# The first matrix of the last feed-forward stage with tokens as standing operand, two of its eight pairs of rows as seven products, and its product turned by TensorE

## The chip, the cores and the metric

The kernel runs on one core of one Trainium2 chip. The metric is the time of one execution on the device in microseconds, the median of several runs. The engines are called PE (TensorE, matmul; PEld its loading of the standing operand), DVE (VectorE), ACT (ScalarE), POOL (GpSimd) and SP (SyncE, which issues the DMA).

## The reference, cut to what matters

Two layers, 256 tokens, width 2048: a retention mixer and a feed-forward stage, then a gated short convolution and a second feed-forward stage, which is the last stage, and a final norm.

```python
def swiglu(h, w_in, w_out):
    a, b = jnp.split(h @ w_in, 2, axis=-1)
    return (jax.nn.silu(a) * b) @ w_out
...
        h = (rms_norm(x, norm2_g[i]) * (1.0 + sc2) + sh2).astype(x.dtype)
        x = (x + g2 * swiglu(h, ffn_w_in[i], ffn_w_out[i])).astype(x.dtype)
    return rms_norm(x, final_g).astype(x.dtype)
```

`w_in` is 2048 x 11264 (5632 columns of a, 5632 of b), `w_out` 5632 x 2048; everything is float32.

## The kernel before, in words

A float32 factor is split in two float32r parts, hi (ACT copies the raw tile into it) and lo (DVE subtracts hi from the raw tile), and a product is made of three: hi x hi, hi x lo, lo x hi. Activations lie as rows of 128 features: `h[k]` has 128 partitions, its hi and lo part, and 256 tokens.

*Products by columns.* `product` (its two matmuls are L422 and L425) takes a 128x128 block of weights as standing operand and streams the 256 tokens of a row past it: one matmul of 512 columns (hi of the weight with hi and lo of the tokens) and one of 256 (lo of the weight). Sixteen rows sum up to one 128-wide column of the output, which lies with its features on partitions.

*Products by tokens.* `by_token` (`thrice`, L435 to L437) takes 128 tokens of a row as standing operand and streams 512 columns of weights past it: six matmuls of 512 columns for a 128x512 block of weights and 256 tokens. The output has tokens on partitions, four banks for two halves of the tokens and two column blocks (`ours`).

*Sevens.* A `Seven` is a pair of rows with two column blocks, seen as a 2x2 product (halves of the tokens and rows, rows and column blocks), made as 7 products in place of 8 (Strassen's form in Winograd's order): 21 matmuls of 512 columns in place of 24. It needs three differences of weights per pair (DVE, L366, L370, L372), four sums of activations per pair (`s1` to `s4`, made once), and four more banks, which `mixed_sums` folds (L1211 to L1214).

*Weights.* All weights lie in DRAM in the order of their use, in chunks of 128x2048 (1 MB). `fetch` brings one into one of three raw buffers (`raw`); `prepare` makes of it two pieces of 128x1024, or for a seven four (1024, 1024, 1024, 512), each a hi (L377, ACT) and a lo (L380, DVE) in one of four buffers. The order of PE is that of the code; on DVE and ACT a scheduler fills in the rest. `ahead_now` says how many pieces are prepared ahead of the one that PE uses: two, and three (`AHEAD + 1`) while the second matrix of the last stage runs. Every engine works its queue in order.

*The last stage.* The 5632 hidden features are 44 tiles of 128, in two parts of 22. A part first makes its 44 columns of the first matrix by columns (`swiglu_in`: a column of a, one of b, `summed` by ACT and DVE, silu, multiplication, `split` into hi and lo: `mid`). In part 0 the first six columns run inside `normed`, which makes `h` beside them, and after each of the next eight a `turn` brings a quarter of x to tokens on partitions (four transposes, L1104, a copy by ACT, L1105). Then the part's 22 rows of the second matrix run by tokens (`last_output`): two groups of 1024 columns, each 11 pairs of rows, of which pairs 1, 4 and 7 are sevens (`SEVEN`), 255 matmuls. `maker` makes the sums of activations for them. At a group's end DVE adds the banks (L1291), multiplies by the gate and adds to x (`gated`, L1171 and L1172); in part 1 ACT sums squares and DVE multiplies by the gain (L1297). In the very last group the last six rows of each column block come apart (`TAIL_ROWS`).

PSUM has eight banks; a group of the second matrix uses all of them.

Of the kernel before, what the change touches and what calls it, by code (L numbers as in the profile page):

```python
# [17 lines left out]
P = 128  # L18
# [22 lines left out]
SEVEN, BESIDE_CB = (1, 4, 7), 88  # L41
# [119 lines left out]
def last_out(ks, last):  # L161

    out = []
    for c in range(0, D, 2 * DV):
        cols, pairs = [c, c + DV], [ks[i : i + 2] for i in range(0, len(ks), 2)]
        rest = []
        if last and c + 2 * DV == D:
            n = TAIL_ROWS // 2
            rest = [Group([col], DV, ks=ks[-TAIL_ROWS:]) for col in cols]
            pairs = pairs[:-n]  # L170
        out.append([(Seven if i in SEVEN else lambda c, k: Group(c, DV, ks=k))(cols, k) for i, k in enumerate(pairs)])
        out[-1] += rest
    return out


LAST_OUT = [last_out(ks, i == 1) for i, ks in enumerate(halves(DFF))]


def in_use_order():
# [10 lines left out]
    for layer in range(DEPTH):  # L190
# [5 lines left out]
        for part in range(2):  # L196
            for g in FFN_IN[part]:
                yield "ffn_w_in", layer, g
            for g in sum(LAST_OUT[part], []) if layer == DEPTH - 1 else FFN_OUT[part]:
                yield "ffn_w_out", layer, g  # L200
# [31 lines left out]
def trunk(ctx: ExitStack, tc: tile.TileContext, x_in, c_in, pos_in, w_mod, cols_in, gain_in, tab_in, w_all, out):  # L232
# [803 lines left out]
    def swiglu_in(layer, part, acc, mid, beside=(), made=split):  # L1036

        pending, done, beside = [], 0, list(beside)
        for i, g in enumerate(FFN_IN[part]):
            pending += [sums(g)] if part or i else normed(acc, layer, 1, g)  # L1040
            while len(pending) >= 2:
                a, b = pending[:2]
                pending = pending[2:]
                s = a()
                g1 = tmp("silu", pool=mpool, bufs=2)
                nc.scalar.activation(g1, s, AF.Silu)
                s = b()
                m = tmp("m", pool=mpool, bufs=2)
                nc.vector.tensor_tensor(m, s, g1, op=ALU.mult)
                made(mid[done], m)  # L1050
                done += 1
            if beside and i:
                beside.pop(0)()
        assert not beside

    def mids():
        return [mpool.tile([P, 2, S], F32R, tag=f"mid{i}", name=name("mid")) for i in range(FT // 2)]

    for part in range(2):
        mid = mids()  # L1060
        swiglu_in(0, part, acc, mid)
# [32 lines left out]
    first_mid = mids()  # L1094
# [20 lines left out]
    def maker(mid):  # L1115
        kept, count = {}, [0]

        def made(dst, m):
            i = count[0]
            count[0] += 1  # L1120
            if i // 2 not in SEVEN:
                split(dst, m)
                return
            kept[i] = m
            if i % 2 == 0:
                split(dst[:, :, :P], m[:, :P])
                return
            split(dst, m)
            (a11, a21), (a12, a22) = [(v[:, :P], v[:, P:]) for v in (kept[i - 1], m)]
            u = tmp("u512", (P, DV), pool=mpool, bufs=3)  # L1130
            s1, s2, s4, s3 = [u[:, n * P : (n + 1) * P] for n in range(4)]
            nc.vector.tensor_tensor(s3, a11, a21, op=ALU.subtract)
            nc.vector.tensor_tensor(s1, a21, a22, op=ALU.add)
            nc.vector.tensor_tensor(s2, s1, a11, op=ALU.subtract)
            nc.vector.tensor_tensor(s4, a12, s2, op=ALU.subtract)
            split(mid[i - 1][:, :, P:], s3)
            split(tokens_sums[SEVEN.index(i // 2)], u[:, : 3 * P])
# [205 lines left out]
```

## Time and profile before

| | |
|---|---|
| median of three runs | 2611.96 us (2611.22 to 2614.11) |
| the profiled execution | 2613.33 us |
| its span, first to last instruction | 2611.6 us |
| PE, PEld, DVE, ACT, POOL busy | 2580.2, 2278.1, 2060.3, 1271.9, 131.6 us |
| HBM read | 685.08 MB, 263 GB/s over the span |
| granted clock of PE | 0.998 |

The profile is of one execution; times are in microseconds from the span's start. A group's mean is the time from start to end of one instruction; matmuls are pipelined, so the next starts before the one ahead has ended, and what a matmul costs is the distance of two starts. L numbers are lines of the kernel before; in the changed kernel the same code has higher numbers (L380 is L405 there, L422 is L447, L435 is L460, L366 is L391, L377 is L402, L487 is L512, L1211 is L1241, L1291 is L1315 in the first matrix and L1363 in the second).

### The profile page before, as it was taken

The page shows a single profiled execution, that of the slowest core. Times are in us where ns is not written, and L with a number is a line of the kernel's source. Part 1 is how long each engine was busy: PE and PEld are TensorE (multiplying, and loading weights), DVE is VectorE, ACT ScalarE, POOL GpSimd, SP SyncE. Part 2 cuts the span into 40 slices and gives each one's busy share as a digit, 9 for nine tenths or more (in the row PEclk, how much of TensorE's full clock was granted, in tenths as well). Part 3 has the DMA queues.
Part 4 walks back from the last instruction along what each step waited for, and adds up shares of the span by engine and source line. Part 5 has one row for each costly group of instructions (what it writes and reads, how often), then busy time and mean ns, then how long its engine had stood idle before and what let it go on. Part 6 is the DMA issues. An engine that isn't in the chain of part 4 may idle for free.

```text
span 2611.6 us, 37574 instructions
## 1 busy us (share of the span) xinstructions
PE 2580.2 (99%) x14831; PEld 2278.1 (87%) x14831; DVE 2060.3 (79%) x2622; ACT 1271.9 (49%) x1824; POOL 131.6 (5%) x232
## 2 busy tenths in 40 slices
PE   7999999999999999999999999999999999999998
PEld 6898889888899888888888898888998888888886
DVE  7988978887698888777778889888965568665678
ACT  5544543444456444344444454444564554445444
POOL 0000000110000001100001000000000000000001
PEclk9999999999999999999999999999999999999999
DMA  9976668867686888787788768887755555555554
GB/s 397 387 289 225 254 250 295 303 248 276 241 307 247 331 320 309 296 300 289 295 296 296 290 233 323 319 292 280 291 180 187 186 210 191 210 186 187 191 209 145
DMA packets 96692, 689.64 MB, mean 264 GB/s; under 512 B 10737, under 2 KB 12161, under 8 KB 13441
## 3 DMA queue, kind: packets, MB, share of 16 engines
q1 hardware_dynamic: 96514, 687.23, 71.4%
q8 instruction: 116, 1.90, 0.3%
q14 instruction: 62, 0.51, 0.1%
HBM read 685.08 MB, written 2.11 MB: 263 GB/s over the span
## 4 chain that ended last, share of the span: by engine, by line
PE 91%; DVE 4%; DMA 3%; issue 1%; ACT 1%; POOL 0%; ACTq 0%; POOLq 0%; DVEq 0%
PE bank L422 40%; PE bank L425 21%; PE bank L436 6%; PE bank L435 6%; PE bank L437 6%; DMA raw<-w_all 2%; PE bank L471 2%; PE bank L470 2%; PE bank L469 2%; DVE lo L380 1%; PE bank L602 1%; PE bank L604 1%; PE bank L603 1%; DMA raw<-w_mod 1%; DVE raw L730 1%
## 5 line engine op out<-in xcount | busy, mean ns | idle before, releaser
L380 DVE TENSOR_TENSOR lo<-raw,hi 128x1024 fp32r<-128x1024 f32 (+1 forms) x924 | 1117.6, 1215 | 461.7 <-ACT hi L377 458.2
L377 ACT CAST hi<-raw 128x1024 fp32r<-128x1024 f32 (+1 forms) x924 | 957.9, 1045 | 1012.8 <-PE bank L422 430.8
L422 PE MATMUL bank<-h,hi 128*128 128x512 f32 x3296 | 1143.9, 390 | 0.0
L425 PE MATMUL bank<-h,lo 128*128 128x256 f32 x3296 | 929.4, 282 | 0.0
L422 PEld LDWEIGHTS bank<-h,hi 128*128 128x128 f32 x3296 | 618.8, 188 | 129.4
L425 PEld LDWEIGHTS bank<-h,lo 128*128 128x128 f32 x3296 | 622.9, 189 | 0.0
L293 DVE SCALAR_TENSOR_TENSOR raw<-raw,cb 128x2048 f32<-128x2048 f32 x160 | 365.8, 2286 | 30.6 <-DMA raw<-w_mod 30.2
L422 PE MATMUL bank<-mid,hi 128*128 128x512 f32 x922 | 319.8, 390 | 0.0
L425 PE MATMUL bank<-mid,lo 128*128 128x256 f32 x922 | 260.1, 282 | 0.9 <-DVE lo L380 0.9
L422 PEld LDWEIGHTS bank<-mid,hi 128*128 128x128 f32 x922 | 173.1, 188 | 36.2
L435 PE MATMUL bank<-hi,h 128*128 128x512 f32 x512 | 201.7, 394 | 1.4 <-DVE rm L714 1.4
L436 PE MATMUL bank<-lo,h 128*128 128x512 f32 x512 | 200.6, 392 | 0.8 <-DVE lo L380 0.8
L437 PE MATMUL bank<-hi,h 128*128 128x512 f32 x512 | 199.7, 390 | 0.0
L425 PEld LDWEIGHTS bank<-mid,lo 128*128 128x128 f32 x922 | 174.3, 189 | 1.2 <-DVE lo L380 1.2
L422 PE MATMUL bank<-rm,hi 128*128 128x512 f32 x496 | 172.5, 390 | 0.0
L471 PE MATMUL bank<-h,lo 128*128 128x256 f32 x512 | 146.5, 286 | 4.4 <-DVE lo L380 4.4
L469 PE MATMUL bank<-h,hi 128*128 128x256 f32 x512 | 145.9, 285 | 3.3 <-ACT h L758 3.3
L470 PE MATMUL bank<-h,hi 128*128 128x256 f32 x512 | 145.9, 285 | 0.7 <-DVE h L759 0.7
L425 PE MATMUL bank<-rm,lo 128*128 128x256 f32 x496 | 139.8, 282 | 0.0
L436 PE MATMUL bank<-lo,mid 128*128 128x512 f32 x304 | 118.5, 390 | 1.3 <-DVE lo L380 1.2
L435 PE MATMUL bank<-hi,mid 128*128 128x512 f32 x304 | 118.4, 389 | 0.0
L437 PE MATMUL bank<-hi,mid 128*128 128x512 f32 x304 | 118.3, 389 | 0.0
(218 smaller groups left out, 2820.4 us busy)
## 6 DMA issues: line engine op xcount, KB each, us to landing
raw<-w_all SPq DMA_DIRECT2D x456, 1024.0 KB, 4.9
raw<-w_mod SPq DMA_DIRECT2D x192, 1024.0 KB, 5.4
x<-x_in SPq DMA_DIRECT2D x4, 512.0 KB, 5.7
out<-xt SPq DMA_DIRECT2D x4, 512.0 KB, 3.0
decay<-tab_in SPq DMA_DIRECT2D x8, 128.0 KB, 2.4
x<-gate_row SPq DMA_DIRECT2D x2, 512.0 KB, 4.6
last_gain<-gain_in SPq DMA_DIRECT2D x1, 1024.0 KB, 4.2
cols<-cols_in SPq DMA_DIRECT2D x1, 152.0 KB, 8.9
```

Source lines behind the costliest of these rows:

```text
L293: nc.vector.scalar_tensor_tensor(raw, raw, 1.0, cb, op0=ALU.mult, op1=ALU.mult, accum_out=total)
L377: nc.scalar.copy(hi, raw)
L380: nc.vector.tensor_tensor(lo, raw, hi.bitcast(F32), op=ALU.subtract)
L422: nc.tensor.matmul(pt, hi, h, start=fresh and k == g.ks[0], stop=False, skip_group_check=True)
L425: nc.tensor.matmul(pt[:, 1, :], lo, h[:, 0, :], start=False, stop=last and k == g.ks[-1], skip_group_check=True)
L435: nc.tensor.matmul(o, hi, w_hi, start=first, stop=False)
L436: nc.tensor.matmul(o, hi, w_lo, start=False, stop=False)
L437: nc.tensor.matmul(o, lo, w_hi, start=False, stop=last)
L469: nc.tensor.matmul(pt, hi, h[:, 0, :], start=first, stop=False, skip_group_check=True)
L470: nc.tensor.matmul(pt, hi, h[:, 1, :], start=False, stop=False, skip_group_check=True)
L471: nc.tensor.matmul(pt, lo, h[:, 0, :], start=False, stop=last, skip_group_check=True)
L602: nc.tensor.matmul(pt, hi, high, start=k == 0, stop=False, skip_group_check=True)
```

## The change

Of the 44 tiles 40 are now made by tokens too, in ten groups of four tiles (a column block of 512 of a, the same of b). Part 0 has 20 tiles, part 1 24 (`LAST_TILES`). Tiles 16 to 19 are still made by columns, six columns in the norm and two after it, with four turns of x after each of the two (`first_rows`). Then `made_in_sums` makes the sums over h for the sevens (pairs 3 and 5 of the eight pairs of rows, `IN_SEVEN`), and four groups follow in part 0, six in part 1. A group's end folds and adds the banks, takes the silu and multiplies, which gives four tiles with tokens on partitions. Ahead of the third pair of the next group (`TURNS_AT`, also if that is one of the second matrix) PE turns them with eight transposes (L1329), ACT and DVE split the result (L1333, L1334), and for the pairs of rows that are sevens in the second matrix `tokens_sums_of` makes the sums. The sevens of the second matrix are pairs 2, 4 and 6 of a group (`OUT_SEVEN`), in part 0 of ten pairs, in part 1 of twelve; part 0's last pairs come in the order 8, 6, 9, 5, 7. `ahead_now` is three from the first group on and is not set back. `h` of the last stage lies 120 elements higher, and small tiles that only take up space have other sizes.

```diff
-SEVEN, BESIDE_CB = (1, 4, 7), 88
+IN_SEVEN, OUT_SEVEN, TURNS_AT, BESIDE_CB, BESIDE_SUMS = (3, 5), (2, 4, 6), 2, 40, 48
+LAST_TILES = 20, 24
...
+def last_in():
+    n, rows = LAST_TILES[0], [(i, [2 * i, 2 * i + 1]) for i in range(KT // 2)]
+    cols = [part * DFF + j * P for j in range(n - 4, n) for part in range(2)]
+    firsts = [Group(cols[:LEAD])] + [Group([c]) for c in cols[LEAD:]]
+    fours = [[*range(0, n - 4, 4)], [*range(n, FT, 4)]]
+    return firsts, [[in_pairs([j * P, DFF + j * P], rows, IN_SEVEN) for j in js] for js in fours]
...
+    h = rows_at(EARLIER)
...
-        swiglu_in(1, part, acc, mid, () if part else turns, maker(mid))
...
+    def tokens_sums_of(a11, a21, a12, a22, third, others):
+        u = tmp("u512", (P, DV), pool=mpool, bufs=3)
+        s1, s2, s4, s3 = [u[:, n * P : (n + 1) * P] for n in range(4)]
+        nc.vector.tensor_tensor(s3, a11, a21, op=ALU.subtract)
+        nc.vector.tensor_tensor(s1, a21, a22, op=ALU.add)
+        nc.vector.tensor_tensor(s2, s1, a11, op=ALU.subtract)
+        nc.vector.tensor_tensor(s4, a12, s2, op=ALU.subtract)
+        split(third, s3)
+        n = 3 * P // len(others)
+        for i, dst in enumerate(others):
+            split(dst, u[:, i * n : (i + 1) * n])
...
+    def made_in_sums():
...
+        for i in IN_SEVEN:
+            both = tmp("u512", (P, 2, S), pool=mpool, bufs=3)
+            for n in range(2):
+                k = 2 * i + n
+                high, low = [h[k].bitcast(F32)[:, v, :] for v in range(2)]
+                nc.vector.tensor_tensor(both[:, n, :], high, low, op=ALU.add)
...
+            tokens_sums_of(*parts(both), h[2 * i][:, :, P:], in_sums[i])
...
-    def last_output(part, c, groups, act, base):
...
+    def gathered(groups, act, base, sums, beside=None, mixed=None):
         ours = {(t, j): flat_bank() for t in range(2) for j in range(2)}
...
+        banks, n = [], len(sums)
         for i, g in enumerate(groups):
+            if beside:
+                beside(i)
+            if i == TURNS_AT and waiting:
+                waiting.pop(0)()
             if isinstance(g, Seven):
                 n -= 1
+                banks = banks or [flat_bank() for _ in range(4)]
...
+    def last_input(groups, pairs, seven):
+        ours, extra = gathered(groups, h, 0, in_sums)
+        for (t, j), pt in ours.items():
+            nc.vector.tensor_tensor(extra[t, j], pt, extra[t, j], op=ALU.add)
+        ms = []
+        for t in range(2):
+            m = extra[t, 0]
+            nc.scalar.activation(m, m, AF.Silu)
+            nc.vector.tensor_tensor(m, m, extra[t, 1], op=ALU.mult)
+            ms.append(m)
+        def turned():
+            for n, (dst, of) in enumerate(zip(pairs, seven)):
+                pt = bank()
+                for i in range(2):
+                    for t, m in enumerate(ms):
+                        c = slice((2 * n + i) * P, (2 * n + i + 1) * P)
+                        nc.tensor.transpose(pt[:, i, t * P : (t + 1) * P], m[:, c], ident)
+                if of is not None:
+                    both = tmp("u512", (P, 2, S), pool=mpool, bufs=3)
+                    nc.scalar.copy(both, pt)
+                nc.scalar.copy(dst[:, :, 0, :], pt)
+                nc.vector.tensor_tensor(dst[:, :, 1, :], pt, dst[:, :, 0, :].bitcast(F32), op=ALU.subtract)
+                if of is not None:
+                    tokens_sums_of(*parts(both), dst[:, 0, :, P:], [of])
+        waiting.append(turned)
...
+        if not part:
+            first_rows(mid[-2:])
+            made_in_sums()
+            ahead_now[0] = AHEAD + 1
+        for i, groups in enumerate(LAST_IN[part]):
...
+            last_input(groups, mid[2 * i : 2 * i + 2], seven)
```

On PE, at the end of a column of part 0 before the change; the first operand is the row of h or the weight that stands or streams, `hi` and `lo` the pieces of weights:

```order
L422 MATMUL bank_3716_20196<-h_97,hi_3708_20162 128x512
L425 MATMUL bank_3716_20196<-h_97,lo_3709_20163 128x256
L422 MATMUL bank_3716_20196<-h_97,hi_3708_20162 128x512
L425 MATMUL bank_3716_20196<-h_97,lo_3709_20163 128x256
L422 MATMUL bank_3722_20239<-h_97,hi_3718_20199 128x512
L425 MATMUL bank_3722_20239<-h_97,lo_3719_20200 128x256
```

And after it, around the transposes of a group's product (`x12` is the tile that holds it now, `tab` the identity), ahead of the third pair of the next group:

```order
L460 MATMUL bank_3522_19114<-hi_3523_19115,h_97 128x512
L461 MATMUL bank_3522_19114<-lo_3524_19116,h_97 128x512
L462 MATMUL bank_3522_19114<-hi_3523_19115,h_97 128x512
L1329 MATMUL bank_3533_19184<-tab_78,x12_76 128x128 x4
L1329 MATMUL bank_3534_19191<-tab_78,x12_76 128x128 x4
L460 MATMUL bank_3519_19111<-hi_3526_19133,h_97 128x512
L461 MATMUL bank_3519_19111<-lo_3527_19134,h_97 128x512
L462 MATMUL bank_3519_19111<-hi_3526_19133,h_97 128x512
L460 MATMUL bank_3521_19113<-hi_3526_19133,h_97 128x512
```

One pair of matmuls for a block of weights has become three for each bank, and between two pairs of rows stand eight transposes.

On DVE, two columns of a and b before the change, from their weights' lo to their split product:

```order
L380 TENSOR_TENSOR lo_3486_18907<-raw_3484_18904,hi_3485_18906 128x1024
L380 TENSOR_TENSOR lo_3488_18927<-raw_3484_18904,hi_3487_18926 128x1024
L481 TENSOR_TENSOR sum_3490_18948<-bank_3476_18854,low_3489_18946 128x256
L380 TENSOR_TENSOR lo_3499_18970<-raw_3497_18967,hi_3498_18969 128x1024
L380 TENSOR_TENSOR lo_3501_18990<-raw_3497_18967,hi_3500_18989 128x1024
L481 TENSOR_TENSOR sum_3493_18954<-bank_3483_18903,low_3492_18952 128x256
L1049 TENSOR_TENSOR m_3494_18956<-sum_3493_18954,silu_3491_18950 128x256
L487 TENSOR_TENSOR mid_3331_18097<-m_3494_18956,mid_3331_18097 128x256
```

And after it, the end of a group of four tiles (`bank` L1315 are its four banks, L1320 the product with the silu), with the lo pieces of the next group between:

```order
L405 TENSOR_TENSOR lo_3573_19379<-raw_3571_19376,hi_3572_19378 128x1024
L405 TENSOR_TENSOR lo_3575_19395<-raw_3571_19376,hi_3574_19394 128x1024
L1315 TENSOR_TENSOR x12_76<-bank_3519_19111,x12_76 128x512
L405 TENSOR_TENSOR lo_3578_19413<-raw_3576_19410,hi_3577_19412 128x1024
L1315 TENSOR_TENSOR u512_3567_19353<-bank_3520_19112,u512_3567_19353 128x512
L1315 TENSOR_TENSOR x12_76<-bank_3521_19113,x12_76 128x512
L1315 TENSOR_TENSOR u512_3568_19354<-bank_3522_19114,u512_3568_19354 128x512
L1320 TENSOR_TENSOR x12_76<-x12_76,u512_3567_19353 128x512
L1320 TENSOR_TENSOR x12_76<-x12_76,u512_3568_19354 128x512
L405 TENSOR_TENSOR lo_3584_19441<-raw_3576_19410,hi_3583_19440 128x1024
L405 TENSOR_TENSOR lo_3587_19459<-raw_3585_19456,hi_3586_19458 128x1024
L391 TENSOR_TENSOR x8_75<-raw_3590_19490 128x1024
```

What was one sum a column with two lo pieces between is now four adds and two multiplications in a row, once for eight columns.

On DVE, where the second matrix of part 0 begins, before the change (the first seven is the second pair):

```order
L380 TENSOR_TENSOR lo_3779_20543<-raw_3777_20540,hi_3778_20542 128x1024
L487 TENSOR_TENSOR mid_3346_18112<-m_3769_20492,mid_3346_18112 128x256
L370 TENSOR_TENSOR raw_3798_20609<-raw_3798_20609,x8_75 128x512
L380 TENSOR_TENSOR lo_3781_20563<-raw_3777_20540,hi_3780_20562 128x1024
L481 TENSOR_TENSOR sum_3783_20584<-bank_3770_20496,low_3782_20582 128x256
L380 TENSOR_TENSOR lo_3800_20613<-raw_3798_20609,hi_3799_20612 128x1024
L372 TENSOR_TENSOR raw_3798_20609<-raw_3798_20609 128x512
L380 TENSOR_TENSOR lo_3802_20617<-x8_75,hi_3801_20616 128x1024
L481 TENSOR_TENSOR sum_3786_20590<-bank_3776_20539,low_3785_20588 128x256
L1049 TENSOR_TENSOR m_3787_20592<-sum_3786_20590,silu_3784_20586 128x256
L380 TENSOR_TENSOR lo_3804_20634<-raw_3798_20609,hi_3803_20633 128x1024
```

And after it, around the transposes that stand ahead of its third pair, which is the first seven; the lo pieces of the pair behind it are the last two rows:

```order
L405 TENSOR_TENSOR lo_3727_20218<-raw_3711_20133,hi_3726_20217 128x512
L1142 TENSOR_TENSOR u512_3720_20196<-u512_3719_20192 128x128
L1143 TENSOR_TENSOR u512_3720_20196<-u512_3719_20192 128x128
L1334 TENSOR_TENSOR mid_3332_18098<-bank_3718_20187,mid_3332_18098 128x2x256
L1144 TENSOR_TENSOR u512_3720_20196<-u512_3720_20196,u512_3719_20192 128x128
L1334 TENSOR_TENSOR mid_3333_18099<-bank_3721_20205,mid_3333_18099 128x2x256
L1145 TENSOR_TENSOR u512_3720_20196<-u512_3719_20192,u512_3720_20196 128x128
L391 TENSOR_TENSOR x8_75<-raw_3733_20249 128x1024
L512 TENSOR_TENSOR mid_3332_18098<-u512_3720_20196,mid_3332_18098 128x128
L512 TENSOR_TENSOR sums_of_tokens_18107<-u512_3720_20196,sums_of_tokens_18107 128x384
L405 TENSOR_TENSOR lo_3730_20230<-raw_3728_20227,hi_3729_20229 128x1024
L405 TENSOR_TENSOR lo_3732_20240<-raw_3728_20227,hi_3731_20239 128x1024
```

The sums of tokens (L1142 to L1145, L512) and the splitting of the turned product (L1334) now stand between the lo pieces of the seven and those of the next pair, and so does the difference of the next seven's weights (L391).

More of the change, by code (lines that the diff above doesn't have):

```diff
@@ L1034, in sums, with silu_times @@
         return lambda dst=None: summed(pt, dst)
[L1036 to L1040, printed above, removed]
+    def silu_times(a, b, g1, m):
+        s = a()
+        nc.scalar.activation(g1, s, AF.Silu)
+        s = b()
+        nc.vector.tensor_tensor(m, s, g1, op=ALU.mult)
+    for part, groups in enumerate(FFN_IN):
+        mid = [mpool.tile([P, 2, S], F32R, tag=f"mid{i}", name=name("mid")) for i in range(FT // 2)]
+        pending, done = [], 0
+        for i, g in enumerate(groups):
+            pending += [sums(g)] if part or i else normed(acc, 0, 1, g)
             while len(pending) >= 2:
-                a, b = pending[:2]
+                g1, m = [tmp(tag, pool=mpool, bufs=2) for tag in ("silu", "m")]
+                silu_times(*pending[:2], g1, m)
                 pending = pending[2:]
[L1044 to L1050, printed above, removed]
-                done += 1
[L1052 to L1061, printed above, removed]
+                split(mid[done], m)
+                done += 1
         acc = output(FFN_OUT[part], mid, (0, GT2), part == 1, (lambda j: scaled_only(1, 0, j)) if part else None)
@@ L1113, in trunk @@
     ] + [mpool.tile([P, 2, 3 * P], F32R, tag="sums_of_tokens", name="sums_of_tokens")]
[L1115 to L1137, printed above, removed]
-        return made
+    def tokens_sums_of(a11, a21, a12, a22, third, others):
[9 more added lines that the diff above has]
+            split(dst, u[:, i * n : (i + 1) * n])
@@ L1141, in trunk, with three @@
+    def three(v):
+        return [v[:, :, n * P : (n + 1) * P] for n in range(3)]
     turns = [lambda t=t, c=c: turn(t, c) for c in range(4) for t in range(2)]
@@ L1188, in added, with sevens @@
             nc.gpsimd.tensor_scalar(some, some, 1.0 / D, EPS, op0=ALU.mult, op1=ALU.add)
[L1190 to L1195 removed]
+    def sevens(g, act, base, sums, ours, banks, first, last):
+        s1, s2, s4 = [[v[:, n, :] for n in range(2)] for v in sums]
+        (a11, s3), (a12, a22) = [[half_of(act[k - base], t) for t in range(2)] for k in g.ks]
         p1, p5, p6, p7 = [(b, first, last) for b in banks]
@@ L1203, in sevens, with mixed_sums @@
         paced(4)
-    def mixed_sums(banks, fold, c):
+    def mixed_sums(banks):
         p1, p5, p6, p7 = banks
@@ L1214, in mixed_sums @@
         nc.vector.tensor_tensor(u2, p5, u2, op=ALU.add)
[L1215 to L1219 removed]
+        return {(0, 0): u1, (1, 0): u3, (1, 1): u4, (0, 1): u2}
     def stored(t):
```

122 lines of the change are left out of this document (75 added, 47 removed).

## The prediction

> **What bounds the kernel now.** I read the page first: the share of each engine, the clock, the chain of waits.
>
> ```profile
> span 2611.6 us, 37574 instructions
> ...
> PE 2580.2 (99%) x14831; PEld 2278.1 (87%) x14831; DVE 2060.3 (79%) x2622; ACT 1271.9 (49%) x1824; POOL 131.6 (5%) x232
> ...
> PEclk9999999999999999999999999999999999999999
> ...
> PE 91%; DVE 4%; DMA 3%; issue 1%; ACT 1%; POOL 0%; ACTq 0%; POOLq 0%; DVEq 0%
> ```
>
> PE is busy 99% of the span at full clock and carries 91% of the chain. The change touches the last feed-forward stage alone, so next stands the view of busy time by stretch, with four: the first matrix's columns of part 0 (38 of its 44; the first six run inside the norm, before 1909), its second matrix, then both of part 1. The columns are the length, PE, weight loads, DVE, ACT, POOL, clock and DMA.
>
> ```profile
> core 0: us, PE busy (x) PEld busy (x) DVE busy (x) ACT busy (x) POOL busy (x), PEclk, DMA share, GB/s
> 1909.00:2123.70 214.70, 214.70 (x1255) 190.65 (x1253) 130.77 (x184) 112.56 (x184) 0.00 (x0) 1.00 0.52 187
> 2123.70:2239.40 115.70, 115.70 (x513) 95.80 (x511) 89.59 (x97) 57.28 (x61) 0.00 (x0) 1.00 0.58 208
> 2239.40:2484.00 244.60, 244.60 (x1412) 216.79 (x1411) 151.47 (x205) 119.51 (x181) 0.00 (x0) 1.00 0.53 191
> 2484.00:2601.00 117.00, 115.70 (x509) 94.87 (x507) 96.39 (x112) 57.79 (x71) 5.91 (x6) 1.00 0.48 173
> ```
>
> In three of the four PE is busy to the last hundredth; in the fourth 1.3 us are missing. So a matmul less here is time less, as long as DVE and ACT, which make the hi and lo pieces that PE reads, keep up. The second matrix's stretches are the model of what the first is to become: twelve sevens are in them already, DVE is at 77 and 82%, and PE waits for nothing in one and 1.3 us in the other.
>
> **The change part by part.** First the price of a matmul: its spacing, not the latency that the groups print as a mean. Part 1 has 44 columns x 16 rows = 704 products of one 128x512 and one 128x256 matmul: 244.60/704 = 0.3474 us each. The second matrix has two groups of 8x24 + 3x21 = 255 matmuls of 128x512 by tokens: 115.70/510 = 0.2269 us each. One 128x128 block of weights costs a product by columns, 0.3474, or six quarters of a matmul by tokens, 0.3403.
>
> *Products against matmuls by tokens.* 40 of the 44 tiles move: 40 x 2 x 16 = 1280 products go, 444.7 us. Ten groups of four tiles come, each 6x24 + 2x21 = 186 matmuls: 1860 x 0.2269 = 422.0 us. Of the 22.7 us saved, 13.6 are the sevens (20 x 3 matmuls) and 9.1 the cheaper form. All of it lies on PE and so on the path.
>
> By the Trainium skill (TensorE: Matmul & The Clock Gate, Back-to-back issue gap) a warm matmul takes 518 cycles at 512 columns and 262 at 256, 134 at 128; by that the two forms cost almost the same, and the net of products, matmuls and transposes would be 24,200 cycles or an estimated 10 us. The trace differs (0.2269 and 0.3474 where that gives 0.216 and 0.325), and its spacings decide.
>
> *Transposes.* Every group turns its product with 8 transposes, 80 in all. The trace has the same form where x is turned, four at a time after each of eight columns (chain rows, start and length):
>
> ```profile
> 1915.03 0.44 PE bank L1104 x4
> ...
> 1956.99 0.44 PE bank L1104 x4
> ```
>
> Seven periods in 41.96 us are 5.994 each; less a column of 16 x 0.3474 = 5.559 this leaves 0.435 for four, 0.109 each. 80 x 0.109 = 8.7 us, on the path. The eight turns of x stay, four after each of two columns instead of one after each of eight.
>
> *DVE and ACT in a new group.* Prices by form in the first second-matrix stretch, and by time where the seven's sums of tokens are made:
>
> ```profile
> L380 DVE TENSOR_TENSOR lo<-raw,hi 128x1024 fp32r<-128x1024 f32 x44 | 53.3, 1221 | 15.9 <-ACT hi L377 15.0
> L377 ACT CAST hi<-raw 128x1024 fp32r<-128x1024 f32 x44 | 45.8, 1054 | 38.6 <-PE bank L437 38.6
> ...
> L366 DVE TENSOR_TENSOR x<-raw 128x1024 f32<-128x1024 f32 x5 | 6.1, 1219 | 2.8 <-DMA raw<-w_all 2.8
> ...
> L380 DVE TENSOR_TENSOR lo<-raw,hi 128x512 fp32r<-128x512 f32 x6 | 4.1, 691 | 5.0 <-ACT hi L377 5.0
> L372 DVE TENSOR_TENSOR raw<-raw 128x512 f32<-128x512 f32 x6 | 4.1, 689 | 0.1
> ...
> L1291 DVE TENSOR_TENSOR x<-bank,x 128x512 f32<-128x512 f32 x3 | 2.1, 686 | 1.1 <-PE bank L437 1.1
> ```
> ```profile
> 1916.10 0.60 ACT L1105 COPY xt<-bank 128x512 f32<-128x512 f32 x1
> ```
> ```profile
> 1924.08 0.29 DVE L1133 TENSOR_TENSOR u<-m,m 128x128 f32<-128x128 f32 x1
> ...
> 1926.62 0.55 DVE L487 TENSOR_TENSOR in_cb<-u,in_cb 128x384 fp32r<-128x384 f32 x1
> ```
>
> A plain pair of rows costs DVE 2 x 1.22 = 2.4 us while PE works 24 x 0.2269 = 5.4. A seven costs it 3 x 1.221 + 0.691 + 1.219 + 2 x 0.69 = 6.95 while PE works 4.8: DVE loses 2.2 us. A group has six plain pairs, two sevens, and 12 operations of 0.686 to fold, multiply and turn the product: 36.8 us, with sums of tokens (six groups of ten: 4 x 0.29 + 0.29 + 0.55) 38.8. PE takes 43.1 with the transposes. So DVE is at 85 to 90%, more than in the model. The worst run is pairs 3, 4, 5 (seven, plain, seven): DVE 16.3 against PE 15.0. Three pieces lie ready when it begins and the folding comes after it, so 1.3 us of lag should be covered. The product is ready in time too: four adds, a silu and two multiplications take some 5 us and have two pairs, 10.9 us. Bounds of the stall per group: 0, and 0.5 if a weight transfer comes late; I take 0.1, 1.0 us in all. ACT has 18 x 1.05 + 2 x 0.6 + up to 7 x 0.6 = 24 us of 43: cover enough. SP issues as many transfers of the same bytes, in another order of columns.
>
> *First group.* Six columns' ends out of the norm had 38 columns to hide behind; now two. From 1909 DVE has these ends and the sums over h (2 x 8 small operations), six lo pieces and one difference, some 23 us at the prices above, until PE begins the third pair at 1909 + 2 x (5.56 + 1.74) + 10.9 = 1934.5: 2.5 us to spare, of which waits for ACT may take more. 0 to 2; I take 0.5.
>
> *Second matrix, first group of part 0.* Here the transposes stand directly ahead of a seven, and the sums of tokens follow. On DVE between the transposes and the lo piece of the next pair: four of 0.29, two of 0.686, 1.219, 0.285, 0.55, 1.22, after one ACT copy of 0.6. Behind these wait in DVE's queue the second seven's difference and all later lo pieces, and in ACT's the casts of the sums. The piece is done some 6.4 us after the transposes' end, and PE wants it after 4.8 + 0.23: 1.4 late, less by the overlap. 0.6 to 1.4; I take 1.1.
>
> *The other three groups of the second matrix.* Their sevens move from pairs 1, 4, 7 to 2, 4, 6: one plain pair between them instead of two. The count of their matmuls is unchanged, 1020, with twelve sevens. From a group's end to its third seven's end DVE has three sevens, four plain pairs (five before) and 12 operations of 0.686 that fold and gate the group before: 38.8 us, 41.3 before; PE has 36.1, 41.5 before. DVE's excess of 2.8 meets a lead of three pieces (3.7) and the 0.08 that neighbouring operations overlap. In the last group 4 more (a gain) come in: 41.6 against 36.1, where 44.0 against 41.5 left the fourth stretch 0.1 us of idle time beside the one wait below. 0 to 1.5 each; I take 1.0 in all.
>
> *Last group's stall.* PE's only real wait of the stage stands in the timeline:
>
> ```profile
> 2592.73 0.39 PE L435 MATMUL bank<-hi,mid 128*128 128x512 f32 x1
> 2594.35 0.50 PE L436 MATMUL bank<-lo,mid 128*128 128x512 f32 x1 [1.23 <-DVE lo L380]
> ```
>
> There the third seven is followed at once by the last rows, and DVE folds and gates (12 x 0.6) ahead of a lo piece. Now two plain pairs stand between, 10.9 us more cover: -1.2 (0 to -1.2). What ends last then is PE again, and the tail after it is the same code.
>
> **Sum:** -22.7 + 8.7 + 1.0 + 0.5 + 1.1 + 1.0 - 1.2 = -11.6 us. The profiled execution took 2613.3 (1.7 beyond its span of 2611.6), so 2601.7 against it; its time stands 1.4 over the median of 2612.0, so 2600.4 for a median.
>
> **Rivals.** *Sevens bound by DVE* (slower): if the three pieces of lead are gone when a seven begins, PE loses up to 2.2 us in each of 20, +44, and the time is 2642. It ends slower than before from 14.0/20 = 0.7 us per seven on. For it: 90% load, and the wait for a transfer below, at the place where DVE goes on behind a difference. Against it: the model's twelve sevens cost PE nothing.
>
> ```profile
> 2536.65 1.23 DVE L366 TENSOR_TENSOR x<-raw 128x1024 f32<-128x1024 f32 x1 [3.73 <-DMA raw<-w_all]
> ```
>
> *Waits at the group's ends* (no change): the operations of a group's end, the transposes and the bank's release cost PE about 0.9 each time, ten times: 2609. For it: banks are eight, and a group now uses ten. Against it: the transposes wait 5 us less than they could.
>
> *h as standing operand is slower than mid.* In retention h stands by tokens too:
>
> ```profile
> L435 PE MATMUL bank<-hi,h 128*128 128x512 f32 x512 | 201.7, 394 | 1.4 <-DVE rm L714 1.4
> ...
> L435 PE MATMUL bank<-hi,mid 128*128 128x512 f32 x304 | 118.4, 389 | 0.0
> ```
>
> 5 ns in one form of three, less in the others; at 2.4 ns over 1860 that is 4.5 us, 2605.
>
> *Transposes at their full length*, 272 ns instead of the spacing:
>
> ```profile
> L1104 PE MATMUL bank<-tab,x x32: 271/272/272, 1914.9 to 1957.2; 128*128 128x128 f32 x32
> ```
>
> Then 80 cost 21.8, the net is about 0, and the time 2613. The periods above speak against it. This is what the Trainium skill (TensorE: Matmul & The Clock Gate, PE-mode transpose) makes of it, some 275 ns each in a kernel, and by that page transposes do not count as work for the clock; the trace has 0.109 and a clock of 1.00.
>
> **How the numbers follow.** Forecast 0.72; h slower 0.07; waits at the ends 0.10; transposes at full length 0.03; bound by DVE 0.06; something that I don't see 0.02. A measurement here tells 0.2%, 5.2 us: faster is below 2606.7. Faster 0.72 + 0.07 + 0.04 of the ends = 0.83, same 0.03 + 0.06 + 0.02 = 0.11, slower 0.06. Range: below, no stall at all and the last wait gone, 2612.0 - 14.0 - 1.2 = 2596.8, rounded to 2596.5; above, all upper bounds at once (2 + 5 + 1.4 + 4.5, the last wait kept) give 2612.0 - 14.0 + 12.9 = 2610.9 and the waits at the ends 2609, both too rare to be kept; what leaves out no more than 2 in 10 is 2608.
>
> **What would show it.** The first matrix's stretches at 43 us a group with PE busy throughout; transposes 0.109 apart; DVE near 88% there; PE's waits for L405's lo at the first sevens of the second matrix and none in the last group. Wrong, if PE waits over 0.5 us for lo or a bank in every new group.

## The result, and the profile after

The changed kernel took 2597.16 us, the median of six runs (2595.98 to 2600.71), against 2611.59 before (2610.23 to 2614.39): 0.9945 of the time before, 95% interval 0.9932 to 0.9958, some 14.4 us less. Forecast were 2600.4, 11.6 us less. The interval means 11 to 18 us less, so the times alone can't tell the forecast from the result; what follows goes by the traces. The same kernel once more, beside other runs (`again`), gave 0.9938 (0.9925 to 0.9950).

The page of the profiled execution (2600.71 us, the longest of its six), in the lines that answer to those of before:

```profile
span 2598.8 us, 36365 instructions
...
PE 2567.0 (99%) x14211; PEld 2241.0 (86%) x14211; DVE 2157.4 (83%) x2702; ACT 1289.4 (50%) x1768; POOL 125.7 (5%) x232
...
PEclk9999999999999999999999999999999999999999
...
PE 84%; DVE 7%; DMA 5%; issue 2%; ACT 1%; ACTq 0%; POOLq 0%; POOL 0%; DVEq 0%; SPq 0%
```

PE still fills 99% at the same clock, with 620 matmuls fewer; DVE works 97 us more and now carries 7% of the chain instead of 4%, PE 84% instead of 91%. In the view of busy time by stretch, from one group's turns to the next, the columns are the length, PE, weight loads, DVE, ACT, POOL, clock and DMA:

```profile
1978.52:2021.59 43.07, 43.07 (x197) 35.74 (x196) 34.88 (x38) 22.55 (x26) 0.00 (x0) 1.00 0.53 196
2021.59:2064.65 43.06, 43.06 (x197) 35.73 (x196) 36.17 (x44) 23.74 (x29) 0.00 (x0) 1.00 0.54 195
```

A group takes PE 43.07 us with no gap, DVE 81 to 84% of it. What PE waits for stands in the timeline, in the last brackets of a row; both places are in the second matrix, in the first group of part 0 and in the last group of part 1:

```profile
2113.91 0.50 PE L461 MATMUL bank<-lo,mid 128*128 128x512 f32 x1 [0.54 <-DVE lo L405]
...
2550.47 0.50 PE L461 MATMUL bank<-lo,mid 128*128 128x512 f32 x1 [0.36 <-DVE lo L405]
...
2552.20 0.51 PE L461 MATMUL bank<-lo,mid 128*128 128x512 f32 x1 [0.76 <-DVE lo L405]
```

The brackets count idle time; what PE loses is the distance of two starts beyond 0.227, 0.8 at 2113 and 1.7 at 2549 to 2552.

For the experiments two lengths are read from each trace by starts: the *stage*, from the last norm's first sum of squares (`ones,acc`) to the last matmul, and the *tail*, from that matmul's start to the end of the last instruction of an engine. The stage begins at 1875.7 to 1882.8 us of the span, from one execution to another without any edit ahead of it, so the stage tells kernels apart better than the whole. Each length is of one execution, though, and the changed kernel's two differ by 1.9 us: a smaller difference counts only where the trace shows the wait that makes it.

| kernel | time / before, 95% | stage us | tail us |
|---|---|---|---|
| before | 1 | 723.0 | 6.55 |
| changed | 0.9945 (0.9932 to 0.9958) | 711.65 | 5.11 |
| changed, `again` | 0.9938 (0.9925 to 0.9950) | 709.8 | 5.11 |
| `no_sevens` | 0.9986 (0.9977 to 0.9995) | 722.4 | 5.10 |
| `three_sevens` | 0.9919 (0.9905 to 0.9932) | 703.9 | 5.11 |
| `four_sevens` | 0.9966 (0.9952 to 0.9979) | 715.5 | 5.11 |
| `turned_twice` | 0.9964 (0.9951 to 0.9976) | 716.9 | 5.11 |
| `spaced` | 0.9931 (0.9917 to 0.9945) | 708.1 | 5.11 |
| `three_spaced` | 0.9914 (0.9900 to 0.9927) | 703.1 | 5.11 |
| `turns_early` | 0.9928 (0.9915 to 0.9940) | 706.3 | 5.11 |
| `tail_as_before` | 0.9946 (0.9934 to 0.9959) | 710.3 | 6.55 |
| `tail_as_after` | 1.0003 (0.9994 to 1.0012) | | |
| `tail_as_after_2` | 1.0000 (0.9991 to 1.0009) | 722.6 | 6.75 |
| `before_both` | 0.9992 (0.9983 to 1.0001) | 721.3 | 5.36 |

The profiled execution of `tail_as_after` took 5737 us, more than twice any other, so no stage and no tail is read from it.

### The profile page after: what moved, and what is told of

The parts are those of the page before. It is cut to its first block, busy times and chain, and to the rows that moved or that the text cites. A ratio compares the mean times of both kernels' runs of the same rounds, so it can differ in the third digit from the quotient of the medians.

```text
span 2598.8 us, 36365 instructions
## 1 busy us (share of the span) xinstructions
PE 2567.0 (99%) x14211; PEld 2241.0 (86%) x14211; DVE 2157.4 (83%) x2702; ACT 1289.4 (50%) x1768; POOL 125.7 (5%) x232
## 4 chain that ended last, share of the span: by engine, by line
PE 84%; DVE 7%; DMA 5%; issue 2%; ACT 1%; ACTq 0%; POOLq 0%; POOL 0%; DVEq 0%; SPq 0%
PE bank L447 25%; PE bank L450 14%; PE bank L461 12%; PE bank L460 12%; PE bank L462 12%; DMA raw<-w_all 4%; DVE lo L405 3%; DMA raw<-w_mod 2%; PE bank L496 2%; PE bank L495 1%; PE bank L494 1%; PE bank L627 1%; PE bank L629 1%; PE bank L628 1%; DVE raw L755 1%
## 5 line engine op out<-in xcount | busy, mean ns | idle before, releaser
L402 ACT CAST hi<-raw 128x1024 fp32r<-128x1024 f32 (+1 forms) x944 | 973.1, 1039 | 1037.0 <-PE bank L462 385.6
L405 DVE TENSOR_TENSOR lo<-raw,hi 128x1024 fp32r<-128x1024 f32 (+1 forms) x944 | 1129.9, 1203 | 347.4 <-ACT hi L402 340.0
L447 PE MATMUL bank<-h,hi 128*128 128x512 f32 x2016 | 699.2, 390 | 0.0
L450 PE MATMUL bank<-h,lo 128*128 128x256 f32 x2016 | 568.4, 282 | 0.0
L447 PEld LDWEIGHTS bank<-h,hi 128*128 128x128 f32 x2016 | 378.3, 188 | 79.2
L460 PE MATMUL bank<-hi,h 128*128 128x512 f32 x1072 | 420.1, 392 | 1.8 <-DVE rm L739 1.8
L461 PE MATMUL bank<-lo,h 128*128 128x512 f32 x1072 | 418.3, 390 | 0.7 <-DVE lo L405 0.7
L462 PE MATMUL bank<-hi,h 128*128 128x512 f32 x1072 | 417.6, 390 | 0.0
L450 PEld LDWEIGHTS bank<-h,lo 128*128 128x128 f32 x2016 | 381.0, 189 | 0.0
L462 PEld LDWEIGHTS bank<-hi,h 128*128 128x128 f32 x1072 | 201.4, 188 | 42.6
L460 PEld LDWEIGHTS bank<-hi,h 128*128 128x128 f32 x1072 | 201.8, 188 | 41.8 <-DVE rm L739 2.4
L461 PEld LDWEIGHTS bank<-lo,h 128*128 128x128 f32 x1072 | 201.9, 188 | 39.9 <-DVE lo L405 1.1
L447 PEld LDWEIGHTS bank<-mid,hi 128*128 128x128 f32 x922 | 173.0, 188 | 36.2
L496 PE MATMUL bank<-h,lo 128*128 128x256 f32 x512 | 146.2, 286 | 5.2 <-DVE lo L405 5.2
```

The costliest lines, as they stand in the source:

```text
L402: nc.scalar.copy(hi, raw)
L405: nc.vector.tensor_tensor(lo, raw, hi.bitcast(F32), op=ALU.subtract)
L447: nc.tensor.matmul(pt, hi, h, start=fresh and k == g.ks[0], stop=False, skip_group_check=True)
L450: nc.tensor.matmul(pt[:, 1, :], lo, h[:, 0, :], start=False, stop=last and k == g.ks[-1], skip_group_check=True)
L460: nc.tensor.matmul(o, hi, w_hi, start=first, stop=False)
L461: nc.tensor.matmul(o, hi, w_lo, start=False, stop=False)
```

## The experiments

**What the sevens bring.** The first edit takes them out of the first matrix; without mixed products the four banks go straight to the silu and the multiplication:

```diff
-IN_SEVEN, ... = (3, 5), ...
+IN_SEVEN, ... = (), ...
...
```

> The ten new groups take all eight pairs of rows in full; the form by tokens, the turns and the second matrix stay. In place of 2 x 42 matmuls in sevens a group has 2 x 48, so 186 matmuls become 192, 60 more in all (the sums of h and the mixing of products go too, so VectorE has less to do). Theory (the path is TensorE, each matmul of 512 columns costs 0.2269 us whatever makes its operands): 60 x 0.2269 = 13.6 us back, 2597.2 + 13.6 = 2610.8, groups 44.4 us apart instead of 43.07, no wait in them. That is level with the kernel before: of the 22.7 us that go out, 9.1 are the form, 8.7 go to the transposes. Rival (the sevens hide less than they save, VectorE holds TensorE up in them): under 7 us more, below 2604. Rival (h as the standing operand is the saving, not the sevens): 2597, no change.

2609.99 us against 2613.28 before. The stage is 722.4, of which PE's wait in the norm takes 0.8 (below). `spaced`, which has two sevens and no wait anywhere, has 708.1, so the sevens are worth 722.4 - 0.8 - 708.1 = 13.5 us: the 13.6 of the theory. Groups:

```profile
2261.13:2305.56 44.43, 44.43 (x203) 36.88 (x202) 21.99 (x20) 18.82 (x21) 0.00 (x0) 1.00 0.53 189
```

44.43 us as expected, and DVE is down to 22. Both rivals fall: with the standing operand h but no sevens the kernel is within 0.2% of the one before.

**How many sevens DVE covers.** Three sevens (their sums lie in tiles that are free by then), then four:

```diff
-IN_SEVEN, ... = (3, 5), ...
+IN_SEVEN, ... = (2, 4, 6), ...      # four_sevens: (2, 3, 5, 6)
```

> Three of the eight pairs in sevens (pairs 2, 4 and 6 instead of 3 and 5). Theory (TensorE sets the pace as long as VectorE's work of a group fits): 6 x 10 = 60 matmuls... 30 matmuls fewer, three in each group: 30 x 0.2269 = 6.8 us, 2590.4, groups 42.39 us apart. VectorE's busy time of a group was 34.9 to 36.2 us; a seven adds about 4.3 (the differences and half the roundings of seven blocks against four), so 39.2 to 40.5 of 42.4, 95%: it fits by its sum. Rival (it fits by the sum but not in time: sevens stand two pairs apart, as in the second matrix, where one wait of 0.8 and one of 1.9 us came up): 0.7 to 1.9 us lost in each of ten groups, 2597 to 2609, with TensorE waiting for the rounding (lo) behind a difference.

2592.73 us. (30 matmuls fewer is the count that holds, three in each of ten groups.) The stage falls from `again`'s 709.8 to 703.9: 6.8 for the matmuls and 0.7 for a wait of `again` that isn't there, less 1.5 for new waits. Of the ten groups five have a small wait (0.3 us) at the pair behind their first seven, where DVE comes from the turned product:

```profile
2252.72:2295.11 42.39, 42.39 (x194) 35.18 (x193) 38.35 (x44) 24.10 (x28) 0.00 (x0) 1.00 0.57 199
2295.11:2337.83 42.72, 42.70 (x194) 35.11 (x193) 39.86 (x50) 25.08 (x31) 0.00 (x0) 1.00 0.55 197
```

So the theory holds up to 93% of DVE (39.86 of 42.72), and the rival only in that 0.3.

> Four of the eight pairs in sevens (2, 3, 5 and 6). TensorE's work of a group falls to 41.7 us. A third seven took VectorE 3.7 us more a group (36.17 to 39.86 in groups that make sums of tokens, 34.89 to 38.35 in the others), so four need 43.5 and 42.0. Theory (VectorE now bounds the first matrix): groups 42.0 to 43.5 us apart and more, TensorE waiting for roundings, 6 x 1.8 + 4 x 0.3 = 12 us given back of the 13.6 gained against two sevens: 2596 at best, 2596 to 2604 with what VectorE still waits for. Rival (roundings run ahead in the plain pairs enough): 2584.

2604.74 us, slower than two, and just beyond the 2596 to 2604 of the theory. Now DVE has no time left:

```profile
2301.33:2346.37 45.04, 42.57 (x191) 34.45 (x190) 44.64 (x56) 26.64 (x33) 0.00 (x0) 1.00 0.50 187
...
2390.34:2435.40 45.06, 42.59 (x191) 34.46 (x190) 44.65 (x56) 26.65 (x33) 0.00 (x0) 1.00 0.51 187
```

DVE is busy 44.64 of 45.04 us, 1.1 us more than the 43.5 expected of such a group, and PE waits for its roundings (the sum in us, the times, the longest):

```profile
PE bank L461 <- DVE lo L405: 10.8, 11, 1.4
```

This sum counts idle time alone. By starts PE loses some 21 us, not 12: the 13.6 us of the fourth and third seven would have made 694.5 out of `spaced`'s 708.1, and the stage is 715.5. The prediction's first rival (sevens bound by DVE) is real; it begins between three and four, where the work of DVE in a group passes that of PE, not at two. In this run the sevens also stand side by side (2 and 3, 5 and 6); no run has four in another order.

**What a transpose costs.**

```diff
-                        nc.tensor.transpose(pt[:, i, t * P : (t + 1) * P], m[:, c], ident)
+                        for _ in range(2):
+                            nc.tensor.transpose(pt[:, i, t * P : (t + 1) * P], m[:, c], ident)
```

> Every transpose of the product is issued twice into the same place of its bank: 80 more transposes, and nothing else. Theory (in the stream of matmuls one takes the 0.109 us from start to start): 80 x 0.109 = 8.7 us more, 2605.9, groups 43.94 us apart. Rival (each one's full length of 0.27 us counts): 80 x 0.27 = 21.8 us more, 2619. Rival (the clock falls with more of them, since a transpose is no work to the throttle): more than 8.7, with a granted clock below 0.99 in the slices of the first matrix.

2605.22 us. The stage is 716.9 without a wait, 8.8 more than `spaced`'s 708.1, also without: 80 x 0.110. A group and the whole first to last of them:

```profile
2257.45:2301.39 43.94, 43.94 (x205) 36.61 (x204) 34.96 (x39) 22.62 (x26) 0.00 (x0) 1.00 0.55 192
1924.19:2470.00 545.81, 545.81 (x2483) 453.93 (x2482) 450.27 (x529) 286.68 (x328) 0.00 (x0) 1.00 0.56 197
```

43.94 as expected and a clock of 1.00, so both rivals are out. The some 275 ns that the Trainium skill (TensorE: Matmul & The Clock Gate, PE-mode transpose) has for a transpose in a kernel agree with the length of one instruction here (272 ns). In a row of them each takes 0.109 us.

**The waits in the second matrix.**

```diff
-    for c in range(0, D, 2 * DV):
+    at = [rows, rows]
+    for c, swapped in ((0, [0, 1, 3, 2, 8, 4, 9, 6, 5, 7]), (1, [0, 2, 1, *range(3, 12)])):
+        if part == c:
+            at[c] = [(i, [first + 2 * i, first + 2 * i + 1]) for i in swapped]
+    for c, rows in zip(range(0, D, 2 * DV), at):
```

> Only the order of pairs in two of the four groups of the second matrix changes: in the first group of part 0 the sevens stand at 3, 5 and 7 instead of 2, 4 and 6, one pair further from the turn of the last product; in the last group of part 1 at 1, 4 and 6 instead of 2, 4 and 6. Theory (TensorE waits there because VectorE comes to a seven with too little lead: behind the turned product's roundings and sums in the one place, two sevens after another in the other): the wait of 0.8 us at 2113 goes, of the 1.9 us at 2549 to 2552 at least the half goes, 2597.2 - 1.7 = 2595.5, at best 2594.5. Rival (VectorE waits there for a transfer, 2.27 us for a piece of the weights ahead of a difference; the transfer is late wherever the seven stands): the waits move with the sevens, 2597.2 and no change.

> The changed kernel once more, unedited, on the chip of the runs beside it. Its profiled execution had waits of TensorE of 1.0 us at 1878 (a norm's sum, ahead of the change), 0.8 at 2113 and 1.7 to 1.9 at 2549 to 2552. Theory (two of them come from that execution: a weight transfer that landed 7.4 us after its issue instead of 4.8 made VectorE late at 2549): the wait at 2113 comes again, the others don't, and from the last norm's first sum to the last matmul's start it takes 709.0 instead of 711.65. Rival (the sevens' spacing in the last group makes them): all come again, 711.6.

`spaced` took 2596.2 us (before: 2613.28) and PE waits nowhere in the stage, so both waits together are 709.8 - 708.1 = 1.6 us of `again`. The timed ratios, 0.9931 and 0.9938, can't tell that apart. That kernel's waits are:

```profile
2110.88 0.50 PE L461 MATMUL bank<-lo,mid 128*128 128x512 f32 x1 [0.53 <-DVE lo L405]
...
2548.17 0.50 PE L461 MATMUL bank<-lo,mid 128*128 128x512 f32 x1 [0.43 <-DVE lo L405]
```

The first came again with the same length, in `tail_as_before` and `three_sevens` too, and the order of pairs removes it. The place alone doesn't make it, though: `no_sevens` and `four_sevens` have the seven in the same place behind the turn, and no wait. The difference stands in DVE's queue. In the four traces with the wait the difference of the next seven's weights (L391) stands between the turned product and the lo piece that PE wants next (L405); in `no_sevens` it stands ahead of the turned product, in `four_sevens` behind the lo pieces. The changed kernel and `four_sevens`:

```profile
2110.82 1.22 DVE L391 TENSOR_TENSOR x<-raw 128x1024 f32<-128x1024 f32 x1
...
2112.63 3.49 DVE L405 TENSOR_TENSOR lo<-raw,hi 128x1024 fp32r<-128x1024 f32 x3
```
```profile
2115.57 1.22 DVE L405 TENSOR_TENSOR lo<-raw,hi 128x1024 fp32r<-128x1024 f32 x1
...
2118.32 1.22 DVE L391 TENSOR_TENSOR x<-raw 128x1024 f32<-128x1024 f32 x1
```

The 1.22 us of L391 are more than the 0.8 that PE loses. (`turned_twice` doesn't wait either; there L391 stands ahead of the turned product, and PE has eight more transposes, 0.87 us.) No run exchanged these two rows alone.

The second wait is 0.7 here, 1.7 in the first profile, so it neither went, as the theory of `again` had it, nor came back whole, as the rival had it. Ahead of it DVE waits for a piece of the weights; the first row is the changed kernel's, the second `again`'s:

```profile
2548.58 1.23 DVE L391 TENSOR_TENSOR x<-raw 128x1024 f32<-128x1024 f32 x1 [2.27 <-DMA raw<-w_all]
```
```profile
2544.55 1.23 DVE L391 TENSOR_TENSOR x<-raw 128x1024 f32<-128x1024 f32 x1 [1.28 <-DMA raw<-w_all]
```

The transfer, issued 47 to 48 us ahead of the last matmul, took 7.4 us from issue to landing in the one, 6.4 in the other and 7.0 in `tail_as_before` (DVE waited 1.8, PE lost 1.3). In `no_sevens`, `three_sevens`, `four_sevens` and `turned_twice`, with the same order of pairs there, it took 4.7 to 4.8, and PE did not wait. So this wait hangs on the landing, as the rival of `spaced` has it: it comes in the three late traces and grows with the delay; whether the other order would take it away with a late landing isn't settled, since in `spaced` and `three_spaced` none there took over 5.3. `again` also settles the 1.0 us at 1878: it isn't there. It is the norm's sum waiting for ACT's square, in `no_sevens` again (0.8), in the other traces not; it belongs to an execution, not to the change.

**Two gains together, and an earlier turn.**

> Three sevens in the first matrix (pairs 2, 4, 6) and the second matrix in the spaced order. Theory (the two gains add): three sevens' 703.9 us from the last norm's first sum to the last matmul less the 0.8 of the wait at the first group of the second matrix, 703.1; some 2592 against 2592.7 of three sevens alone. Rival (VectorE, at 93% in the first matrix now, has no lead left when the second matrix begins, so the wait only moves): 703.9 and no gain.

2590.33 us against 2612.43, and 703.1: the 0.8 is gone and nothing came in its place. This has the lowest ratio of the study, though its interval overlaps that of `three_sevens`; that the 0.8 is gone stands in the trace.

```diff
-IN_SEVEN, OUT_SEVEN, TURNS_AT, BESIDE_CB, BESIDE_SUMS = (3, 5), (2, 4, 6), 2, 40, 48
+IN_SEVEN, OUT_SEVEN, TURNS_AT, BESIDE_CB, BESIDE_SUMS = (2, 4, 6), (2, 4, 6), 1, 40, 48
...      # the rest as in three_spaced
```

> Three sevens in the first matrix and the spaced order of the second, with the product of a group turned one pair into the next group instead of two (so a pair lies between the turns and the first seven). Theory (five waits of 0.2 to 0.3 us behind the turned product's roundings and sums go, and the product is ready in time: four additions, a silu and a multiplication, some 4.5 us, against a pair's 5.4): 703.1 - 1.4 = 701.7 us from the last norm's first sum to the last matmul, 2589. Rival (VectorE takes roundings between, and the product isn't ready after 5.4 us): TensorE waits at each of ten turns by up to 1 us, 703 to 712 us, 2590 to 2599.

2594.62 us, and a stage of 706.3, 3.2 us longer. PE loses some 0.2 us at each of the ten turns, and the five waits behind the first seven grew from 0.3 to 0.55 instead of going. The rival holds, at its low end: the product is not quite ready after 5.4 us. In the one of the five looked at, at 2298.8, a difference of weights (L395, 1.22 us) now stands in DVE's queue right ahead of the lo piece that PE waits for; that this makes all five longer is not shown.

**The tail.** The changed kernel's tail is 1.44 us shorter, though the code is the same; DVE's queue, which the scheduler fills, has another order. In the changed kernel half 0's sum and scaling (L1250, L1261, L1259) stand ahead of half 1's multiplication (L1209):

```profile
2588.18 0.21 DVE L1250 TENSOR_SCALAR rs<-total,sums 128x1 f32<-128x1 f32 x1 [0.86 <-ACT u L1213]
2589.06 0.48 DVE L1261 TENSOR_SCALAR xt<-xt,rs 128x512 f32<-128x512 f32 x1 [0.67 <-POOL rs L1254]
2589.46 0.74 DVE L1259 SCALAR_TENSOR_TENSOR xt<-xt,rs,last_gain 128x512 f32<-128x512 f32 x1
2590.13 0.68 DVE L1209 TENSOR_TENSOR u<-bank,x 128x512 f32<-128x512 f32 x1
```

In the kernel before that multiplication (L1177) stands first and waits for PE, with half 0 behind it:

```profile
2601.26 0.69 DVE L1177 TENSOR_TENSOR u<-bank,x 128x512 f32<-128x512 f32 x1 [1.02 <-PE bank L437]
2601.86 0.20 DVE L1224 TENSOR_SCALAR rs<-total,sums 128x1 f32<-128x1 f32 x1
```

The order was put back in the changed kernel, and put in by hand in the kernel before:

```diff
+                if tail:             # tail_as_before, on the changed kernel
+                    with tc.manual_schedule(engines={nc.tensor.engine, nc.vector.engine, nc.scalar.engine}):
+                        last = g.cols[0] // DV
+                        added(0, last, ours[0, j], True)
+                        u = multiplied(last, ours[1, j])
+                        stored(0, lambda: added(1, last, ours[1, j], False, u))
+                        nc.scalar.activation(u, at(xt[1], last), AF.Square, accum_out=total[:, 1, last : last + 1])
+                        stored(1)
...
+                if tail:             # tail_as_after, on the kernel before
+                    hand = tc.manual_schedule(engines={mybir.EngineType.PE, mybir.EngineType.DVE})
+                    hand.__enter__()
                 for t in range(2):
...
+                if tail:
+                    hand.__exit__(None, None, None)
```

In the first `stored(0, ...)` puts half 1's addition behind half 0's sum; in the second the loop over the halves keeps the order of the code.

> The changed kernel, with the end of VectorE's and ScalarE's queues put as in the kernel before: half 1's multiplication, which waits for TensorE, and then its addition, ahead of half 0's scaling, and half 1's square behind half 0's scaling on ScalarE. Theory (this order alone makes the tail longer): from the last matmul's start to the last instruction 6.5 us instead of 5.1, and 1.4 us more than the changed kernel's 0.9938 of the time before, 0.9944. Rival (the tail got shorter because of something else): 5.1 us and 0.9938.

A tail of 6.55 instead of 5.11: in the changed kernel the order is worth the whole 1.44. (The time, 0.9946 with 0.9934 to 0.9959, agrees with the theory's 0.9944 and can't exclude the rival's 0.9938.)

```profile
2586.38 0.69 DVE L1209 TENSOR_TENSOR u<-bank,x 128x512 f32<-128x512 f32 x1 [2.66 <-PE bank L462]
2586.98 0.20 DVE L1255 TENSOR_SCALAR rs<-total,sums 128x1 f32<-128x1 f32 x1
```

> The kernel before, with one edit: in the last group's last block VectorE takes its operations in the order of the code, so that half 0's sum and scaling stand ahead of half 1's multiplication, which waits for TensorE; so they stand in the changed kernel. Theory (the 1.4 us by which the tail after the last matmul's start is shorter in the changed kernel come from this order alone): that stretch falls from 6.55 to 5.1 us, 0.9994 of the time before. Rival (the tail is shorter because of something else, such as where the last weights land): 6.5, no change.

> The kernel before with the changed kernel's order at the end of VectorE's queue, once more, since the execution profiled of it the first time was a disturbed one of 5.7 ms, and the timed ones gave 1.0003 of the time before. Theory (the order gives 1.4 us): 5.1 us from the last matmul's start to the end. Rival: 6.5. The profile also shows a second time how long TensorE waits for a rounding in the last group of the kernel before (1.4 and 0.1 us at 2592.7 in its first profile): the same if the place of the sevens makes it, another length if a late transfer does.

1.0003 (0.9994 to 1.0012) and 1.0000, in the second with a tail of 6.75: in the kernel before the same order gives nothing. There DVE is late: PE's wait in the last group came again (1.4 us at the same matmul). It doesn't come from a late transfer: the 7.7 and 6.6 us of two transfers issued at 2529 and 2533 in the first profile were 5.3 and 4.8 in this one. That it comes with the place of the seven the next run shows. DVE reaches half 0's sum at 2600.33, 0.26 us after the last matmul's start (2600.07), and half 1's bank 2.2 after it:

```profile
2600.33 0.21 DVE L1224 TENSOR_SCALAR rs<-total,sums 128x1 f32<-128x1 f32 x1 [0.86 <-ACT u L1181]
...
2602.27 0.68 DVE L1177 TENSOR_TENSOR u<-bank,x 128x512 f32<-128x512 f32 x1
```

In the changed kernel half 0's sum stood 1.4 us ahead of it (2588.18 against 2589.55). So the kernel before got both, the order and a third seven at place 6 of its last group instead of 7:

```diff
+        if rest:
+            numbered[6:8] = numbered[7], numbered[6]
```

> The kernel before with two edits in its last group: the third seven stands at 6 instead of 7 (two plain pairs ahead of the last rows instead of one), and VectorE takes the end in the changed kernel's order. Alone the order gave nothing (6.75 us from the last matmul to the end), because VectorE, late behind TensorE's wait of 1.4 us, was still at half 0 when half 1 was ready. Theory (the short tail needs both, the order and a VectorE in time): the wait of 1.4 and 0.1 us goes and the tail falls to 5.1: 3.0 us less, 0.9989. Rival (the tail is set elsewhere): the wait goes, the tail stays at 6.5 or more: 1.5 us less, 0.9994.

2611.67 us against 2613.27. The trace has the theory: no wait of PE in the stage (721.3, 1.75 less than before) and a tail of 5.36, 1.2 of the 1.44 less. The timed ratio, 0.9992 (0.9983 to 1.0001), agrees with 0.9989 but can't tell it from the rival's 0.9994.

## Why the prediction was right, and where not

The time lies in the range, near its low end: 14.4 us came where 11.6 were forecast. By its steps:

- *Products against matmuls and transposes*: -22.7 + 8.7 = -14.0 forecast. Ten groups of 43.07 are 430.7. A product by columns takes 0.3467 from start to start in the trace of before (the 704 of part 1 from 2239.40 to 2483.48), so the 1280 take 443.8: -13.1. The prediction's 0.3474 is a little too high, because its stretch of 244.60 ran 0.5 us into the second matrix; the cheaper form is worth 8.2, not 9.1. `no_sevens` gives 13.5 of the 13.6, `turned_twice` 8.8 of the 8.7.
- *Rate of matmuls with h standing*: 0.227 between starts; that rival is out. So is the full length of transposes, and the waits at the groups' ends: there are none.
- *Stalls in the new groups*, +1.0 forecast: none with two sevens. It was sized from DVE's sum and a lead of three pieces, and that sum was a little high (36.8 to 38.8 forecast, 34.9 to 36.2 measured). *First group*, +0.5: nothing. There is no wait, and the turns of x cost the same in their new place (3.5 us with the delay of the matmul behind them, 3.6 before).
- *Second matrix, first group*, +1.1: 0.8, at the matmul named. The next seven's difference, which the prediction counted among the rows ahead of the lo piece, seems to decide: in the two kernels where it stands elsewhere there is no wait, but no run moved this row alone.
- *The other three groups*, +1.0 in all: none in two, 0 to 1.7 in the last. I took it for a shortage of DVE's time; in the seven traces with this order of pairs there it comes with a late transfer.
- *Last group's stall*, -1.2: the wait is gone, and as starts go it was 1.5. The prediction's sign, no wait in the last group, did not come all the same, because of the one just named. A smaller wait of the kernel before (0.33 at 2551.5), of which the prediction said nothing, went too; `tail_as_after_2` doesn't have it either, so it belongs to that execution.
- Summed with the measured sizes: -13.1 + 0.8 + 0.7 - 1.5 - 0.3 = -13.4 for `again`, whose stage is 13.2 shorter; with 1.7 in the last group and 1.0 in the norm -11.4 for the first profile, which has -11.4.
- *The tail*: "the tail after it is the same code" is the step that failed. It was 1.44 us shorter, half of the 2.8 between forecast and time. The code is the same, but its order on DVE isn't, and the last rows of DVE in the two programs would have told it. The price could have been read too: DVE's 1.02 us of idle time behind PE, with half 0's scaling behind it, and ACT's square of half 1 behind that.

The rest has two signs: the stalls, 3.6 forecast (0.1 for each new group among them), were 0.8 to 2.5, and the last group's two old waits were 0.6 more than the 1.2 forecast, while the products saved 0.9 less. The time came near the forecast partly by luck, since these misses and the tail's 1.44 cancel in part; the path (PE, by starts of matmuls) and the counts on it were right. The first bound of the range, "no stall at all and the last wait gone", was thus not the lowest possible.

## What to carry to other kernels

Where PE fills the span, work by starts between matmuls: the count of matmuls and the transposes came out within 0.2 us of the sum, the cheaper form within 0.9. The stalls of the helping engine are read by its work in a group against PE's (93% gave nearly none, above 100% gave back more than the gain), and each place where a wait may stand needs its own two numbers, the lead and the landing of the transfer. When code is moved, compare the order of the unchanged code at the program's end as well: a scheduler may turn two rows there, and one row that waits ahead of one that doesn't cost 1.4 us in the kernel whose VectorE was in time, and nothing in the one where it was late.

## What was not expected of the hardware

The median transfer of 1 MB of weights takes 4.8 us from issue to landing in this stage, the slowest up to 7.7. The view of transfers in the stretch of the late one of `again`, and in the same place of `three_sevens`, in time:

```profile
q1 hardware_dynamic: 190, 1.29, 47.8%
q8 instruction: 1, 0.02, 1.2%
...
raw<-w_all SPq DMA_DIRECT2D x1, 1024.0 KB, 6.4
```
```profile
q1 hardware_dynamic: 192, 1.31, 54.1%
...
raw<-w_all SPq DMA_DIRECT2D x1, 1024.0 KB, 4.8
```

In all three late ones of this place (`again`, the changed kernel's first profile and `tail_as_before`, whose programs differ only in the tail) a packet of an instruction queue (0.02 MB) stands in the stretch, in the four punctual ones none. Over the whole stage of the thirteen traces with a stage in the table, 83 of 488 transfers with such a packet between issue and landing took over 5.3 us, and 23 of 919 without one. So most transfers with a packet are in time, and some without are late, but late ones stand beside packets far more often. That fetching code delays one of the transfer's parts would fit; no run made or removed such a packet on purpose, so it stays open.
